# Gate/up projections of a SwiGLU layer as 2x2 block products with seven multiplications, and the down projection in pieces between them

## The chip, the cores and the metric

The kernel runs on one core of a Trainium2 chip. The metric is the device time of one execution in microseconds. In the texts, PE is TensorE, DVE is VectorE, ACT is ScalarE and SP is SyncE, whose queue issues the loads.

## The reference

A decoder trunk of two layers over 512 tokens and 1024 channels, in float32. Layer 0 mixes tokens by retention and pooling, layer 1 by a convolution module; each is followed by a SwiGLU sub-layer, and a final RMS norm ends the trunk. The change concerns SwiGLU alone (2816 hidden features):

```python
def rms_norm(x, g):
    y = x32 * lax.rsqrt(jnp.mean(x32 * x32, axis=-1, keepdims=True) + EPS)
    return (y * g).astype(x.dtype)

def swiglu(h, w_gate, w_up, w_down):
    return (jax.nn.silu(h @ w_gate) * (h @ w_up)) @ w_down

for layer in range(DEPTH):
    ...
    h = h + swiglu(rms_norm(h, ffn_norm_g[layer]), ffn_w_gate[layer], ffn_w_up[layer], ffn_w_down[layer])
return rms_norm(h, final_norm_g)
```

## The kernel before

Activations lie feature-major: X holds 8 tiles of 128 features by 512 tokens. A float32 product is made from fp32r parts. Each operand is split into a high part, a cast on ACT (L180 for weights, L230 for hidden tiles), and a low part, the difference to the original on DVE (L183, L231). A product is then three matmuls, high by high, high by low and low by high (`mm3`, L197 to L200).

Weights come in chunks of at most 128 x 2048 floats. `start_load` loads a chunk on SP's queue into `wr` (two buffers), `split_load` makes `wh` and `wl`, and `chunk(name, j)` splits one chunk ahead of the one it returns. A gate/up chunk holds 8 tiles of input features, each with 128 gate columns and 128 up columns, for one tile of hidden features; there are 22 of them. `feature_major` (L202) runs through it: 8 input tiles, two halves, three matmuls of 512 columns each, 48 in all, into one PSUM tile `ps_gu` of two banks. PSUM has three such pairs (`pair`, L302), and tiles for small results beside them.

`hidden` (L536) evacuates the pair: DVE multiplies both halves by the spread inverse rms (L539), ACT applies silu to the gate half (L540), DVE multiplies by the up half (L541), and the result is split into `hh` and `hl`. The inverse rms itself comes from token sums after chunk 0 (`inv_rms`, L294) and is spread over the partitions during chunk 1.

The hidden features go in two halves of 11 tiles. After 11 chunks the down projection of that half follows: four pairs of output tiles, each 2 x 11 x 3 matmuls of 512 columns into `ps_dn`, added to X on DVE (`add_residual`, L305). After layer 0's second half the add also prepares the next layer's input (`norm_input`, L241). After layer 1's, `finish` (L574) does the last pair in halves of 256 tokens, turns X back to token-major by transposes, and scales and stores the rows.

The order of instructions on each engine comes from a scheduler, in a few stretches from the order of the code (`manual_schedule`). An instruction waits for others by counters, at most some per instruction; each engine runs its instructions in order.

Of the kernel before, what the change touches and what calls it, by code (L numbers as in the profile page):

```python
# [22 lines left out]
DFF = 2816  # L23
FT = DFF // P
FH = FT // 2
CW = 31
EPS = 1e-6
CHUNK = 2048
# [52 lines left out]
def trunk(ctx: ExitStack, tc: tile.TileContext, a: dict):  # L81
# [17 lines left out]
    def V(name, i=0, n=1):  # L99
        o, _ = _VEC[name]  # L100
        return vec[:, o + i:o + i + n]
# [24 lines left out]
    for layer in range(2):  # L126
        if layer:
            plan += [("w_pw1", i, 8, 256) for i in range(8)]
            plan += [("w_pw2", i, 8, 256) for i in range(4)]
        for half in range(2):  # L130
            plan += [(f"w_gu{layer}", half * FH + i, 8, 256) for i in range(FH)]
            plan += [(f"w_dn{layer}", half * 8 + i, FH, 128) for i in range(8)]
    ready = {}
    state = {"started": 0, "next": 0, "used": 0}

# [2 lines left out]
    def start_load():  # L138
# [19 lines left out]
                nc.sync.dma_start(raw[:, s], a[name][j][:, s])  # L158
        raws[i] = raw

    def split_load(pieces=1, apart=False):
# [10 lines left out]
        wh = wp.tile([P, CHUNK], F32R, tag="wh", name=f"wh{i}")  # L172
        wl = wp.tile([P, CHUNK], F32R, tag="wl", name=f"wl{i}")
        ready[(name, j)] = (wh[:, :n].rearrange("p (k c) -> p k c", c=c),
                            wl[:, :n].rearrange("p (k c) -> p k c", c=c))
        pieces = KT if i == 0 else 4 if i == 1 else pieces
        step = n // pieces
        for k in range(pieces):
            s = slice(k * step, (k + 1) * step)
            nc.scalar.copy(wh[:, s], raw[:, s])  # L180
            if apart:
                yield
            nc.vector.tensor_tensor(wl[:, s], raw[:, s], wh[:, s].bitcast(F32), ALU.subtract)  # L183
            if i == 0:
                norm_input(k, vg[:, k:k + 1], None, xin)
            yield
# [118 lines left out]
    def add_residual(j, ps, gain=None, acc=None, bias=None):  # L305

        xx = X[:, 2 * j:2 * j + 2, :]
        if bias is None:
            nc.vector.tensor_tensor(xx, ps, xx, ALU.add)  # L309
# [12 lines left out]
    def both(ap):  # L322
        return ap.unsqueeze(1).to_broadcast([P, 2, S])
# [200 lines left out]


    def ffn(layer, acc, gain):
        with tc.tile_pool(name=f"hp{layer}", bufs=FH + 2, reuse_waits="tile") as hp:
            return ffn_in(layer, acc, gain, hp)

    def ffn_in(layer, acc, gain, hp):  # L530
        nacc = None
        row = {}
        for half in range(2):
            hh, hl = [], []

            def hidden(ps):  # L536
                t = wk.tile([P, 2, S], F32, tag="gu", name="gu")
                s = wk.tile([P, S], F32, tag="act", name="act")
                nc.vector.tensor_tensor(t, ps, both(row["rb"]), ALU.mult)  # L539
                nc.scalar.activation(s, t[:, 0, :], AF.Silu)  # L540
                nc.vector.tensor_tensor(s, s, t[:, 1, :], ALU.mult)  # L541
                hh.append(hp.tile([P, S], F32R, tag="hh", name=f"hh{len(hh)}"))
                hl.append(hp.tile([P, S], F32R, tag="hl", name=f"hl{len(hl)}"))
                split(hh[-1], hl[-1], s)

            pss = []
            for f in range(FH):
                wh, wl = chunk(f"w_gu{layer}", half * FH + f)
                pss.append(pair(f"ps_gu{f}"))
                late = {}  # L550
                if not half and f == 1:
                    r = inv_rms(acc)
                    late = {5: lambda: row.update(rb=spread(r, "rms"))}
                feature_major(pss[-1], wh, wl, xgh, xgl, between=late)
                while pss and row:
                    hidden(pss.pop(0))
            if half:
                nacc = new_acc()
            for j in range(3 if gain is None and half else 4):
                ps = pair(f"ps_dn{j}")  # L560
                for i in range(2):
                    down(ps, i, *chunk(f"w_dn{layer}", half * 8 + 2 * j + i), hh, hl)
                add_residual(j, ps, gain, nacc)
        if gain is None:
            finish(hh, hl, nacc)
        return nacc

    def down(ps, i, wh, wl, hh, hl, cols=FULL, between={}):
        for f in range(FH):
            if f in between:  # L570
                between[f]()
            mm3(ps[:, i, cols], wh[:, f, :], wl[:, f, :], hh[f][:, cols], hl[f][:, cols], f == 0, f == FH - 1)

    def finish(hh, hl, acc):  # L574

        A, B = HALVES
        for k in range(6):
            nc.scalar.activation(X[:, k, :], X[:, k, :], AF.Identity, scale=V("fin_g", k))
        ps = pair("ps_dn3")
        pts, stats = {}, {}  # L580

        def tail_add(i, cols):

            x = X[:, 6 + i, cols]
            nc.vector.tensor_tensor(x, ps[:, i, cols], x, ALU.add)
            sq = wk.tile([P, S // 2], F32, tag="sq", name="sqf")
            nc.scalar.activation(sq, x, AF.Square)
            nc.vector.tensor_scalar_mul(x, x, V("fin_g", 6 + i))
            return sq

        def turn(t, ks):

            if t not in pts:
                pts[t] = pair(f"ps_x{t}")
            for k in ks:
                nc.tensor.transpose(pts[t][:, k // 4, k % 4 * P:(k % 4 + 1) * P], X[:, k, t * P:(t + 1) * P], ident)

        def sums(cols, sqs):
# [18 lines left out]
        w6 = chunk("w_dn1", 14)  # L617
        w7 = chunk("w_dn1", 15)
        down(ps, 0, *w6, hh, hl, A)
        s6 = tail_add(0, A)  # L620
        down(ps, 1, *w7, hh, hl, A)
        s7 = tail_add(1, A)

        def at3():
            sums(A, [s6, s7])
            turn(0, range(8))

        def at6():
            turn(1, range(8))

        down(ps, 0, *w6, hh, hl, B, {3: at3, 6: at6})
        scale_rows(A)
        s6 = tail_add(0, B)
        down(ps, 1, *w7, hh, hl, B)
        s7 = tail_add(1, B)
        sums(B, [s6, s7])
        for t in (2, 3):
            turn(t, range(8))
        scale_rows(B)
# [331 lines left out]
```

## Time and profile before

| | |
|---|---|
| median of 3 runs | 1117.32 us (1116.86 to 1117.76) |
| the profiled execution | 1117.25 us |
| its span | 1115.1 us |
| granted PE clock, mean | 0.995 |
| DVE busy | 580.1 us in 784 instructions |
| ACT busy | 334.8 us in 383 instructions |
| load of a gate/up chunk, issue to landing | 4.8 us for 1024 KB, 44 of them |
| HBM read | 100.34 MB, 92 GB/s over the span |

The profile is one execution taken by the hardware profiler. Its span is what lies between the first and the last instruction; 2.15 us of the execution's time lie outside it. A row of a group gives busy time, the mean of one in nanoseconds, and the idle time of the engine just before. Matmuls are pipelined, so the length of one matmul in a row is longer than the distance to the next start. Layer 0's FFN has its first chunk from about 187 us to 198 us, layer 1's from about 738 us to 749 us; both end with the start of the next part, at 548 us and with the tail.

### The profile page before, as it was taken

The numbers are of one execution on the slowest core, as the hardware profiler recorded it, in microseconds if no ns is written. First come the engines' busy times: TensorE is split into PE (matmuls) and PEld (weight loads), VectorE is DVE, ScalarE is ACT, GpSimd is POOL, SyncE is SP. The second block draws the span as 40 slices with busy tenths as digits, with TensorE's granted clock in tenths as the row PEclk, the third lists the DMA queues.
The fourth block names the chain that finished last, engine by engine and source line by source line (L and its number), as shares of the span: only waits on it lengthen the run. The fifth ranks groups of instructions, "written<-read, shape, count | busy, mean of one in ns | idle before, by whom it ended". The sixth has DMA issues, their size and how long they took to land.

```text
span 1115.1 us, 12874 instructions
## 1 busy us (share of the span) xinstructions
PE 1100.3 (99%) x5504; PEld 896.3 (80%) x5504; DVE 580.1 (52%) x784; ACT 334.8 (30%) x383; POOL 20.1 (2%) x10
## 2 busy tenths in 40 slices
PE   9999999999999999999999999999999999999996
PEld 6877878888888888888886577988888888888886
DVE  7875646444432353434469857854444324344333
ACT  6622143223221132223332123432322112222331
POOL 0000100000000000000000410000000000000000
PEclk9999999999999999999999999999999999999998
DMA  8322113222223322222426562233221232231212
GB/s 280 124 93 96 38 44 139 82 101 88 78 78 128 113 81 108 89 79 81 149 76 118 100 137 77 76 114 110 79 102 57 99 136 93 101 110 55 91 65 76
DMA packets 24744, 109.89 MB, mean 99 GB/s; under 512 B 2800, under 2 KB 6768, under 8 KB 15984
## 3 DMA queue, kind: packets, MB, share of 16 engines
q1 hardware_dynamic: 24112, 108.03, 30.0%
q8 instruction: 43, 0.70, 0.3%
q10 hardware_dynamic: 576, 1.05, 0.3%
q14 instruction: 13, 0.11, 0.0%
HBM read 100.34 MB, written 2.10 MB: 92 GB/s over the span
## 4 chain that ended last, share of the span: by engine, by line
PE 91%; DVE 6%; issue 1%; DMA 1%; ACT 1%; SPq 0%; DVEq 0%; ACTq 0%
PE ps_gu L198 14%; PE ps_gu L199 14%; PE ps_gu L200 14%; PE ps_dn L200 7%; PE ps_dn L198 7%; PE ps_dn L199 7%; DVE d L693 3%; PE ps_c L701 2%; PE ps_pw L198 1%; PE ps_wo L199 1%; PE ps_qk L199 1%; PE ps_qk L200 1%; PE ps_wo L200 1%; PE ps_qk L198 1%; PE ps_pw L199 1%; PE ps_pw L200 1%
## 5 line engine op out<-in xcount | busy, mean ns | idle before, releaser
L180 ACT CAST wh<-wr 128x2048 fp32r<-128x2048 f32 (+4 forms) x116 | 179.8, 1554 | 505.9 <-PE ps_gu L199 240.1
L198 PE MATMUL ps_gu<-xgh,wh 128*128 128x512 f32 x704 | 274.4, 390 | 0.0
L200 PE MATMUL ps_gu<-xgh,wl 128*128 128x512 f32 x704 | 274.1, 389 | 0.0
L199 PE MATMUL ps_gu<-xgl,wh 128*128 128x512 f32 x704 | 274.1, 389 | 0.0
L183 DVE TENSOR_TENSOR wl<-wr,wh 128x2048 fp32r<-128x2048 f32 (+4 forms) x116 | 214.2, 1850 | 100.6 <-ACT wh L180 100.2
L539 DVE TENSOR_TENSOR gu<-ps_gu,bc_rms 128x1024 f32<-128x1024 f32 x44 | 53.9, 1225 | 210.8 <-PE ps_gu L200 202.7
L200 PEld LDWEIGHTS ps_gu<-xgh,wl 128*128 128x128 f32 x704 | 132.2, 188 | 27.5
L198 PEld LDWEIGHTS ps_gu<-xgh,wh 128*128 128x128 f32 x704 | 132.2, 188 | 27.3
L199 PEld LDWEIGHTS ps_gu<-xgl,wh 128*128 128x128 f32 x704 | 132.2, 188 | 27.2
L198 PE MATMUL ps_dn<-hh,wh 128*128 128x512 f32 (+1 forms) x374 | 141.3, 378 | 0.0
L200 PE MATMUL ps_dn<-hh,wl 128*128 128x512 f32 (+1 forms) x374 | 140.9, 377 | 0.0
L199 PE MATMUL ps_dn<-hl,wh 128*128 128x512 f32 (+1 forms) x374 | 140.9, 377 | 0.0
L198 PEld LDWEIGHTS ps_dn<-hh,wh 128*128 128x128 f32 x374 | 70.4, 188 | 12.9
L199 PEld LDWEIGHTS ps_dn<-hl,wh 128*128 128x128 f32 x374 | 70.4, 188 | 12.9
L200 PEld LDWEIGHTS ps_dn<-hh,wl 128*128 128x128 f32 x374 | 70.4, 188 | 12.8
L198 PE MATMUL ps_pw<-xgh,wh 128*128 128x512 f32 (+1 forms) x160 | 56.6, 354 | 0.0
L230 ACT CAST hh<-act 128x512 fp32r<-128x512 f32 x44 | 27.3, 621 | 96.4 <-DVE act L541 96.4
L199 PE MATMUL ps_pw<-xgl,wh 128*128 128x512 f32 (+1 forms) x160 | 55.9, 349 | 0.0
L200 PE MATMUL ps_pw<-xgh,wl 128*128 128x512 f32 (+1 forms) x160 | 55.8, 349 | 0.0
L309 DVE TENSOR_TENSOR X<-ps_dn,X 128x1024 f32<-128x1024 f32 x15 | 18.4, 1225 | 66.2 <-PE ps_dn L200 66.2
L231 DVE TENSOR_TENSOR hl<-act,hh 128x512 fp32r<-128x512 f32 x44 | 30.5, 693 | 30.2 <-ACT hh L230 30.2
L701 PE MATMUL ps_c<-R,dg 128*32 128x512 f32 (+1 forms) x512 | 43.9, 496 | 1.6 <-DMA R<-u 1.6
(188 smaller groups left out, 1181.5 us busy)
## 6 DMA issues: line engine op xcount, KB each, us to landing
wr<-in_w_gu SPq DMA_DIRECT2D x44, 1024.0 KB, 4.8
wr<-in_w_dn SPq DMA_DIRECT2D x32, 704.0 KB, 4.0
wr<-in_w_pw SPq DMA_DIRECT2D x12, 1024.0 KB, 4.9
R<-u SPq DMA_DIRECT2D x16, 270.0 KB, 8.0
wr<-in_w_o SPq DMA_DIRECT2D x4, 1024.0 KB, 4.7
X<-in_xT SPq DMA_DIRECT2D x8, 256.0 KB, 4.3
wr<-in_w_qk SPq DMA_DIRECT2D x2, 1024.0 KB, 5.1
wr<-in_w_u SPq DMA_DIRECT2D x2, 1024.0 KB, 4.8
```

Of the source, the lines that this page charges most:

```text
L180: nc.scalar.copy(wh[:, s], raw[:, s])
L183: nc.vector.tensor_tensor(wl[:, s], raw[:, s], wh[:, s].bitcast(F32), ALU.subtract)
L198: nc.tensor.matmul(out, lhsT=wh, rhs=xh, start=start, stop=False)
L199: nc.tensor.matmul(out, lhsT=wh, rhs=xl, start=False, stop=False)
L200: nc.tensor.matmul(out, lhsT=wl, rhs=xh, start=False, stop=stop)
L230: nc.scalar.copy(h, src)
L231: nc.vector.tensor_tensor(l, src, h.bitcast(F32), ALU.subtract)
L309: nc.vector.tensor_tensor(xx, ps, xx, ALU.add)
L539: nc.vector.tensor_tensor(t, ps, both(row["rb"]), ALU.mult)
L693: nc.vector.scalar_tensor_tensor(o, us[j][:, at], V("dwc", CW * j + q), o, ALU.mult, ALU.add)
L701: nc.tensor.matmul(ps[32 * i:32 * i + 32, :n], lhsT=dgs[j][:, i, g, :], rhs=Rs[j][:, i, 4 * g + cols.start:4 * g + cols.stop], start=g == ...
```

## The change

Of each layer's 22 gate/up chunks, 3 stay as they are (`NSTD`). The other 19 are computed as a 2x2 block product. One side is the weight chunk: its two halves of input features (4 tiles each) by gate and up. The other is the input: the same halves of features by two halves of 256 tokens. Seven products of blocks (4 tiles, 3 matmuls each, 256 columns, 84 matmuls) take the place of eight. Three use plain blocks of weights, four use sums of blocks.

Added work, per layer once: `prepare` makes the sums of input blocks `th`, `tl` (ACT scales, DVE subtracts, both split), and `last_operand` overwrites half of four input tiles with the last one. Per chunk: `plain_hi`, `plain_lo` (L594, L600) split the plain blocks; `add_up` (L606) makes the four sums of weight blocks in place in the loaded chunk, one after the other; `sums_hi`, `sums_lo` (L615, L620) split them.

The products gather in two PSUM tiles, `ps_xz` with x in its first bank and z in its second, and `ps_y`. x is accumulated through four products, and between them ACT copies what it holds at that point to SBUF (`sn`); DVE adds these up (L755 adds z, L758, L762) and scales by the inverse rms (L764, L765, L768).

The down projection is cut into six groups of 3, 4, 4, 3, 4 and 4 hidden tiles. Each group by each of the four output pairs is one piece, 24 in all. One piece follows each of the 19 block-product chunks, for the group whose hidden tiles are done; 5 pieces come at the end. A piece's sum is subtracted from X by `add_piece` at the start of the next cycle (before: one add for 11 tiles). Each piece loads its own slice of the down weights (`load_dn`, two DMAs) and splits it (`dn_hi`, `dn_lo`, L636, L641). Loads of chunks (`load_gu`) and pieces go through SP's queue. PE, DVE and ACT run in the order of the code throughout the FFN. In layer 1 the last two pieces are done in token halves with the tail.

The core of the diff, the cycle of one chunk:

```diff
+        def cycle(f, before):
+            s = f - first
+            xz, y = pair(f"ps_xz{f}"), pair(f"ps_y{f}")
+            x, z, y = xz[:, 0, :HS], xz[:, 1, :HS], y[:, 0, :HS]
...
+            product(x, plain_of(f, 0), whole(0, A), True)
+            nc.scalar.copy(sn[0][:, 0, :], x)
+            before()
+            product(y, sum_of(f, 1), part(0), True)
+            dn_hi(s, 0)
+            nc.scalar.copy(sn[1][:, 0, :], y)
+            product(x, sum_of(f, 2), part(1), False)
+            dn_hi(s, 1)
+            nc.scalar.copy(sn[0][:, 1, :], x)
+            plain_lo(f + 1)
+            product(z, plain_of(f, 1), whole(4, A), True)
+            add_up(f + 1)
+            dn_lo(s)
+            load_dn(s + 2)
+            nc.vector.tensor_tensor(g[:, 0, A], z, sn[0][:, 0, :], ALU.add)
+            product(x, sum_of(f, 3), part(2), False)
+            nc.scalar.copy(sn[1][:, 1, :], x)
+            nc.vector.tensor_tensor(g[:, 1, B], sn[1][:, 1, :], sn[1][:, 0, :], ALU.add)
+            sums_hi(f + 1, 1)
+            sums_hi(f + 1, 3)
+            product(y, sum_of(f, 4), whole(4, B), False)
+            nc.vector.tensor_tensor(g[:, 0, B], y, sn[0][:, 1, :], ALU.add)
+            sums_hi(f + 1, 2)
+            nc.vector.tensor_tensor(g[:, 0, :], g[:, 0, :], rb, ALU.mult)
+            nc.vector.tensor_tensor(g[:, 1, B], g[:, 1, B], rb[:, B], ALU.mult)
+            sums_hi(f + 1, 4)
+            product(x, plain_of(f, 2), whole(0, B), False)
+            nc.vector.tensor_tensor(g[:, 1, A], x, rb[:, A], ALU.mult)
+            nc.scalar.activation(sil, g[:, 0, :], AF.Silu)
+            sums_lo(f + 1)
+            load_gu(f + 3)
+            plain_hi(f + 2)
+            ps = piece(s)
+            if f == FT - 1:
+                weights(s + 1)
+            store_hidden(f, sil, g[:, 1, :])
+            return lambda: add_piece(s, ps)
```

What each chunk asks of the sums and products, and the way in:

```diff
+        def add_up(f):
+            if f < FT:
+                a11, a21, a12, a22 = [block(raw_g[f], half, r) for half in range(2) for r in range(2)]
+                for o, i in ((a22, a21), (a21, a11), (a11, a22), (a12, a11)):
+                    nc.vector.tensor_tensor(o, o, i, ALU.add)
...
+        def product(out, w, xs, first):
+            h, l = w
+            for k in range(4):
+                xh, xl = xs(k)
+                for n, (u, v) in enumerate(((h, xh), (h, xl), (l, xh))):
+                    nc.tensor.matmul(out, lhsT=u[:, k, :], rhs=v, start=first and k == 0 and n == 0,
+                                     stop=k == 3 and n == 2, skip_group_check=True)
...
+        feature_major(p0, *w, xgh, xgl)
+        prepare(0)
+        w = chunk(f"w_gu{layer}", 1)
+        load_gu(NSTD)
+        r = inv_rms(acc)
+        prepare(1)
+        p1 = pair("ps_gu1")
+        feature_major(p1, *w, xgh, xgl, between={5: lambda: row.update(rb=spread(r, "rms"))})
+        prepare(2)
+        prepare(3)
+        hidden(0, p0)
+        w = chunk(f"w_gu{layer}", 2, 0)
+        load_gu(NSTD + 1)
+        p2 = pair("ps_gu2")
+        feature_major(p2, *w, xgh, xgl)
+        plain_hi(NSTD)
+        plain_lo(NSTD)
+        add_up(NSTD)
+        for i in (1, 2, 3, 4):
+            sums_hi(NSTD, i)
+        hidden(1, p1)
+        sums_lo(NSTD)
+        load_gu(NSTD + 2)
+        last_operand()
+        plain_hi(NSTD + 1)
+        hidden(2, p2)
+        before = lambda: None
+        for f in range(NSTD, FT):
+            before = cycle(f, before)
```

How this moves instructions shows in the built order. First DVE, in the middle of layer 0's FFN. Before, a chunk has four instructions there: the gain on the PSUM pair `ps_gu`, the low part `wl` of the next weights, the product with the silu, and the low part `hl`:

```order
L539 TENSOR_TENSOR gu<-ps_gu_1913,bc_rms 128x1024
L183 TENSOR_TENSOR wl_1974<-wr_1971,wh_1973 128x2048
L541 TENSOR_TENSOR act<-act,gu 128x512
L231 TENSOR_TENSOR hl_1968<-act,hh_1967 128x512
L539 TENSOR_TENSOR gu<-ps_gu_1977,bc_rms 128x1024
```

Now one cycle, from add_piece (X and `ps_dn`) over the next chunk's plain low parts (here `wl`), its four sums (`wg`), the piece's low weights (`dl0d`) and the add of z (L755) to the low part of `hl`:

```order
L311 TENSOR_TENSOR X<-X,ps_dn_2087 128x1024
L600 TENSOR_TENSOR wl_2084<-wg_6_1928,wh_2083 128x1024
L600 TENSOR_TENSOR wl_2084<-wg_6_1928,wh_2083 128x512
L606 TENSOR_TENSOR wg_6_1928<-wg_6_1928 128x4x128 x4
L641 TENSOR_TENSOR dl0d_2144<-dr_2_1874,dh0d_2143 128x2x384
L755 TENSOR_TENSOR gu<-ps_xz_2111,sn_2113 128x256
L758 TENSOR_TENSOR gu<-sn_2114 128x256
L762 TENSOR_TENSOR gu<-ps_y_2112,sn_2113 128x256
L764 TENSOR_TENSOR gu<-gu,bc_rms 128x512
L765 TENSOR_TENSOR gu<-gu,bc_rms 128x256
L768 TENSOR_TENSOR gu<-ps_xz_2111,bc_rms 128x256
L620 TENSOR_TENSOR wl_2199<-wg_6_1928,wh_2198 128x2048
```

The evacuation, which stood first after a chunk, is now in pieces, and the first of them stands behind eight instructions that belong to the piece before, the next chunk and this piece's weights.

Second, PE at the change from z's product to x's third product, in the next cycle (`ps_xz` holds both, `th` and `tl` are sums of input blocks). The wait at the head of the third product is for DVE, and its count is reached with L755 of the same cycle; the wait at the head of z's product is for ACT's copy of x:

```order
L682 MATMUL ps_xz_2264<-xgh_1460,wh_2083 128x256 [waits Activation_49]
L682 MATMUL ps_xz_2264<-xgl_1461,wh_2083 128x256
L682 MATMUL ps_xz_2264<-xgh_1460,wl_2084 128x256
...
L682 MATMUL ps_xz_2264<-xgh_1482,wl_2084 128x256
L682 MATMUL ps_xz_2264<-th_0_1572,wh_2198 128x256 [waits DVE_49]
L682 MATMUL ps_xz_2264<-tl_0_1573,wh_2198 128x256
```

Before, the same place of PE's order has one chunk after another with no wait between them but for the buffers:

```order
L198 MATMUL ps_gu_2041<-xgh_1342,wh_1973 128x512
L199 MATMUL ps_gu_2041<-xgl_1343,wh_1973 128x512
L200 MATMUL ps_gu_2041<-xgh_1342,wl_1974 128x512
L198 MATMUL ps_gu_2041<-xgh_1460,wh_1973 128x512
L199 MATMUL ps_gu_2041<-xgl_1461,wh_1973 128x512
```

So PE now stops inside a chunk for two other engines, which it did not.

Third, DVE on the way into layer 0's FFN, after the last input tile (`xgl_1483`) is made. Before, the next work after four small clears for the convolution is the inverse rms (`ms` and on):

```order
L227 SCALAR_TENSOR_TENSOR xgl_1483<-X,vec,xgh_1482 128x512
L256 TENSOR_TENSOR acc<-acc,sq_1486 128x512
L661 MEMSET u_3780 128x31
L661 MEMSET u_3787 128x31
L661 MEMSET u_3849 128x31
L661 MEMSET u_3918 128x31
L296 TENSOR_SCALAR ms<-ps_ms 128x4
```

Now a prepare (`xr`, then `t4` in the row L666, then `tl`) and the split of chunk 2 (`wl_1579`) stand ahead of it:

```order
L229 SCALAR_TENSOR_TENSOR xgl_1483<-X,vec,xgh_1482 128x512
L258 TENSOR_TENSOR acc<-acc,sq_1486 128x512
L661 TENSOR_TENSOR xr_1565<-xg_1564 128x2x256
L663 SCALAR_TENSOR_TENSOR xr_1565<-xr_1565,xg_1564 128x256
L666 SCALAR_TENSOR_TENSOR t_0_1570<-xr_1565,xg_1564 128x256
L233 TENSOR_TENSOR tl_0_1573<-xr_1565,th_0_1572 128x768
L185 TENSOR_TENSOR wl_1579<-wr_1576,wh_1578 128x2048
L298 TENSOR_SCALAR ms<-ps_ms 128x4
```

So the inverse rms comes behind five instructions more, and three more prepares follow it before the evacuation of chunk 0.

More of the change, by code (lines that the diff above doesn't have):

```diff
@@ L25 @@
 FH = FT // 2
+NSTD = 3
+GROUPS = [range(h + i, h + j) for h in (0, FH) for i, j in ((0, 3), (3, 7), (7, 11))]
 CW = 31
@@ L129, in trunk @@
             plan += [("w_pw2", i, 8, 256) for i in range(4)]
-        for half in range(2):
-            plan += [(f"w_gu{layer}", half * FH + i, 8, 256) for i in range(FH)]
-            plan += [(f"w_dn{layer}", half * 8 + i, FH, 128) for i in range(8)]
+        plan += [(f"w_gu{layer}", i, 8, 256) for i in range(NSTD)]
     ready = {}
@@ L159, in start_load, with split_tiles @@
         raws[i] = raw
+    def split_tiles(i):
+        return [wp.tile([P, CHUNK], F32R, tag=f"{t}{i % 2}", name=f"{t}{i}", bufs=1) for t in ("wh", "wl")]
     def split_load(pieces=1, apart=False):
@@ L303, in pair, with add_residual @@
         return pmm.tile([P, 2, S], F32, tag="mm", name=name)
-    def add_residual(j, ps, gain=None, acc=None, bias=None):
+    def add_residual(j, ps, gain=None, acc=None, bias=None, sign=ALU.add):
         xx = X[:, 2 * j:2 * j + 2, :]
         if bias is None:
-            nc.vector.tensor_tensor(xx, ps, xx, ALU.add)
+            nc.vector.tensor_tensor(xx, xx, ps, sign)
         else:
@@ L526, in ffn @@
     def ffn(layer, acc, gain):
[L527 to L531, printed above, removed]
-        row = {}
[L533 to L563, printed above, removed]
-        if gain is None:
-            finish(hh, hl, nacc)
-        return nacc
@@ L568, in down @@
[L568 to L574, printed above, removed]
+        with tc.tile_pool(name=f"fx{layer}", bufs=1, reuse_waits="tile") as fx, \
+                tc.tile_pool(name=f"fg{layer}", bufs=1, reuse_waits="tile") as fg, \
+                tc.tile_pool(name=f"fy{layer}", bufs=1, reuse_waits="tile") as fy, \
+                tc.manual_schedule(engines={mybir.EngineType.PE, mybir.EngineType.DVE, mybir.EngineType.Activation}):
+            gap = fg.tile([P, 16], F32, name=f"gap{layer}")
+            nc.vector.memset(gap[:1, :1], 0.0)
+            return ffn_in(layer, acc, gain, fx, fy)
```

253 lines of the change are left out of this document (225 added, 28 removed).

## The prediction

> **What bounds the kernel now.** I read the page first: busy times, then the chain that ended last.
>
> ```profile
> PE 1100.3 (99%) x5504; PEld 896.3 (80%) x5504; DVE 580.1 (52%) x784; ACT 334.8 (30%) x383; POOL 20.1 (2%) x10
> ...
> PE 91%; DVE 6%; issue 1%; DMA 1%; ACT 1%; SPq 0%; DVEq 0%; ACTq 0%
> ```
>
> PE is busy for 99% of the span and is 91% of the chain; DVE has half its time free. Next the waits, for PE alone. The longest is its first row:
>
> ```profile
> PE ps_c L701 <- DMA R<-u: 1.6, 1, 1.6
> ```
>
> So PE waits nowhere for long, and taking matmul time away pays only if it still waits nowhere afterwards. What a matmul costs on the path is the distance between starts, since its 390 ns overlap the next one. The timeline of PE near the end has both widths side by side, 512 columns and then 256 (start, length):
>
> ```profile
> 1071.63 0.39 PE L198 MATMUL ps_dn<-hh,wh 128*128 128x512 f32 x1
> ...
> 1083.64 0.39 PE L200 MATMUL ps_dn<-hh,wl 128*128 128x512 f32 x1
> 1083.87 0.28 PE L198 MATMUL ps_dn<-hh,wh 128*128 128x256 f32 x1
> ...
> 1087.70 0.28 PE L200 MATMUL ps_dn<-hh,wl 128*128 128x256 f32 x1
> ```
>
> 53 steps in 12.01 us are 0.2266 us for 512 columns; 32 steps in 3.83 us are 0.1197 us for 256, a little over half.
>
> **Part 1, the matmuls.** A chunk of gate/up is 48 matmuls of 512 columns now, 48 x 0.2266 = 10.88 us. As seven block products it is 7 x 4 x 3 = 84 of 256 columns, 10.05 us. The down projection keeps its matmuls. So 0.83 us a chunk: 19 chunks give 15.7 us a layer, 31.4 us in both. An eighth fewer multiplications has become 7.6%, because narrow matmuls cost more per column.
>
> **Part 2, one cycle of a chunk.** The other engines' durations, from the groups by form (mean ns of one after the comma):
>
> ```profile
> L539 DVE TENSOR_TENSOR gu<-ps_gu,bc_rms 128x1024 f32<-128x1024 f32 x44 | 53.9, 1225 | 210.8 <-PE ps_gu L200 202.7 <-ACT bc_rms L291 8.1
> L309 DVE TENSOR_TENSOR X<-ps_dn,X 128x1024 f32<-128x1024 f32 x15 | 18.4, 1225 | 66.2 <-PE ps_dn L200 66.2
> L183 DVE TENSOR_TENSOR wl<-wr,wh 128x2048 fp32r<-128x2048 f32 x66 | 151.3, 2292 | 44.7 <-ACT wh L180 44.5
> L183 DVE TENSOR_TENSOR wl<-wr,wh 128x1024 fp32r<-128x1024 f32 x2 | 2.4, 1220 | 0.0
> L183 DVE TENSOR_TENSOR wl<-wr,wh 128x512 fp32r<-128x512 f32 x8 | 5.2, 686 | 0.1
> L585 DVE TENSOR_TENSOR X<-ps_dn,X 128x256 f32<-128x256 f32 x4 | 1.7, 421 | 7.2 <-PE ps_dn L200 7.2
> L667 DVE SCALAR_TENSOR_TENSOR u<-gu,vec,act 128x256 f32<-128x256 f32 x4 | 1.9, 484 | 1.3 <-ACT act L665 1.2
> L180 ACT CAST wh<-wr 128x2048 fp32r<-128x2048 f32 x66 | 126.2, 1912 | 329.3 <-PE ps_gu L199 192.2 <-PE ps_dn L199 28.9 <-PE ps_g L449 28.0
> L180 ACT CAST wh<-wr 128x1024 fp32r<-128x1024 f32 x2 | 2.0, 1042 | 0.0
> L180 ACT CAST wh<-wr 128x512 fp32r<-128x512 f32 x8 | 4.5, 612 | 3.8 <-PE ps_p L219 3.8
> L540 ACT ACTIVATE act<-gu 128x512 f32<-128x512 f32 x44 | 27.5, 626 | 3.6 <-DVE gu L539 2.6
> L226 ACT ACTIVATE xgh<-X,vec 128x512 fp32r<-128x512 f32 x24 | 17.2, 716 | 1.9 <-DVE X L309 1.6
> L291 ACT COPY mus<-ps_mu 128x256 f32<-128x256 f32 x2 | 0.7, 372 | 8.5 <-PE ps_mu L287 8.5
> ```
>
> How they follow each other is in the timelines: DVE back to back, DVE on its own result, ACT back to back, DVE after PE, and PE after a wait.
>
> ```profile
> 192.89 0.75 DVE L227 SCALAR_TENSOR_TENSOR xgl<-X,vec,xgh 128x512 fp32r<-128x512 f32 x1
> 193.55 0.69 DVE L256 TENSOR_TENSOR acc<-acc,sq 128x512 f32<-128x512 f32 x1
> ...
> 199.74 0.16 DVE L269 TENSOR_TENSOR rs_t<-rs_t,rs_h 128x4 f32<-128x4 f32 x1
> 199.94 0.16 DVE L270 SCALAR_TENSOR_TENSOR rs_y<-rs_t,rs_y 128x4 f32<-128x4 f32 x1
> ```
>
> ```profile
> 714.49 1.14 ACT L180 CAST wh<-wr 128x512 fp32r<-128x512 f32 x2
> ```
>
> ```profile
> 221.37 0.39 PE L200 MATMUL ps_gu<-xgh,wl 128*128 128x512 f32 x1
> 221.80 1.22 DVE L539 TENSOR_TENSOR gu<-ps_gu,bc_rms 128x1024 f32<-128x1024 f32 x1 [4.84 <-PE ps_gu L200]
> ```
>
> ```profile
> 685.78 0.39 PE L221 MATMUL ps_p<-zh,wh 128*128 128x256 f32 x1 [0.60 <-DVE zh L756]
> 686.00 0.28 PE L222 MATMUL ps_p<-zh,wl 128*128 128x256 f32 x1
> ```
>
> Independent work on DVE starts 0.09 us before the last ends; dependent work 0.04 after. A second 512 cast on ACT adds 0.52. A hop between engines is 0.03 to 0.05, counted from the end of the last matmul, and PE's first step after a wait is 0.22.
>
> The kernel text decides the rest. x and z are the two halves of one PSUM tile, and in the built order waits go by tile: z's product waits for ACT's copy of x, and x's third product waits for DVE's add of z (L755). DVE reaches that add only behind add_piece, the low parts of the next chunk's plain blocks, four block sums each waiting for the one before, and the low part of the piece's weights. So I count from the end of one add of z to the next.
>
> - PE restarts at 0.05; x's third product takes 0.22 + 11 x 0.12 = 1.54, y's second 1.44 (to 3.03, results 3.19), x's fourth 1.44 (to 4.47, results 4.63). Then the piece: 18 matmuls (3 chunks) to 8.55, or 24 (4 chunks) to 9.91; results 0.16 later.
> - ACT: four casts of sums, which wait for y's second: 3.22 + 3 x 0.52 + 0.61 = 5.4.
> - DVE: adds and gains up to 5.08, low part of the sums 5.43 to 7.72, product with the silu to 8.33; ACT's cast of hh to 8.98; low part hl to 9.70.
> - DVE then: add_piece from 9.62 (3 chunks) or, waiting for PE, 10.10 (4). To the end of the next add of z: 1.14 + 1.14 + 0.73 + 3 x 0.73 + 0.60 + 0.87 (1.14 for 4 chunks, 0.95 and 1.22 less the overlap) + 0.42 = 7.1 or 7.3.
>
> The period is 16.7 us (3 chunks) or 17.4 us (4). PE's own work is 84 x 0.1197 + 18 x 0.2266 = 14.13, or 15.49. PE waits 2.5 or 1.95 us in every cycle. From chunk 3 to chunk 21 there are 18 such steps, 8 with 3 chunks and 10 with 4, the last 0.4 shorter because nothing is prepared: 8 x 2.55 + 10 x 1.95 - 0.4 = 39.5 us a layer. DMA adds no wait: load_gu has a cycle for its transfer, and load_dn's two smaller ones on SP stand ahead of it.
>
> **Part 3, the way in.** The first chunks now also carry four prepare steps, in order on DVE and ACT. The timelines and the chain where layer 0's FFN starts:
>
> ```profile
> 197.93 1.90 ACT L180 CAST wh<-wr 128x2048 fp32r<-128x2048 f32 x1 [6.00 <-PE ps_gu L199]
> ...
> 206.80 0.59 ACT L291 COPY bc_rms<-ps_rms 128x512 f32<-128x512 f32 x1 [6.97 <-PE ps_rms L287]
> ```
>
> ```profile
> 198.94 0.16 DVE L296 TENSOR_SCALAR ms<-ps_ms 128x4 f32<-128x4 f32 x1 [4.54 <-PE ps_ms L279]
> ...
> 203.21 0.16 DVE L270 SCALAR_TENSOR_TENSOR rs_y<-rs_t,rs_y 128x4 f32<-128x4 f32 x1
> ...
> 749.77 0.16 DVE L296 TENSOR_SCALAR ms<-ps_ms 128x4 f32<-128x4 f32 x1 [5.12 <-PE ps_ms L279]
> ```
>
> ```profile
> 198.12 0.79 PE ps_ms L279 x8
> ...
> 205.87 0.89 PE ps_rms L287 x8
> ```
>
> Chunk 2's weights can be split only when chunk 0 is done: ACT to 199.83, DVE to 202.2; the twelve small steps of rsqrt (4.4 us between the quoted two, of which the 2.2 us of a split stood among them) to 204.4. A prepare is 0.69 + 2 x 0.52 = 1.73 on DVE, then ACT's cast (0.83, between 512 and 1024) and the next two scaled copies (0.62 + 0.72), because its two buffers rotate. Prepare 1 to 206.1, ACT's rms copy and copies to 208.7, prepare 2 to 210.4, prepare 3 to 213.8, its low part to 215.1. hidden(0), 1.2 + 0.63 + 0.75 + 0.62 + 0.69 with hops, to 219.1; plain low parts to 221.2; four sums to 224.1; hidden(1) to 228.0; low part of the sums to 230.3. PE finished chunk 2 at 198.91 + 2 x 10.88 + 0.89 = 221.56, and y's first product stands until 230.3. Then four low parts of the last operand (231.6), hidden(2) (235.6, with ACT's copy of x behind it), plain low parts (237.3), sums (240.1), piece weights (241.0), and the add of z ends at 241.4. PE's own work would have had z at 221.56 + 5.75 = 227.3: 14.1 us late. Layer 1 has the same rows 550.8 us later, so again 14.1.
>
> **Part 4, the ends.** In the last four pieces of layer 0 (5.44 us of PE each) DVE has an add, two norms and a split, about 6 us; the low weights come 0.6 late twice: 1.2. In layer 1 piece 23's weights queue behind the squares and come 2.0 late, and the tail has a 512 add for a 256 one and a second square: 0.65.
>
> **Sum.** 2 x (-15.7 + 14.1 + 39.5) + 1.2 + 2.65 = +79.7 us. The profiled execution took 1117.25 us, its span 1115.1 and 2.15 around it; the median is 1117.32. So 1117.25 + 79.7 = 1197 us.
>
> **Bounds.** The uncertain terms are not PE's. Below: if the hidden split never delays the next add_piece, a 3-chunk cycle has only the stretch behind the piece's end, 8.71 + 7.1 = 15.8, and if a 4-chunk one is 0.25 shorter, the 18 steps cost 30; with a way in of 11 us that is 2 x (-15.7 + 11 + 30) = +51, 1168. Above: 12 hops of the loop each 0.06 longer are 0.7 a cycle, 25 us: 1222.
>
> **The rivals.**
> *The wait is not there, faster.* If x's third product can run while z is read, PE waits only on the way in. Without the wait at L755 the copy of x frees PE at 235.2 there, and z, x, y, x and the piece follow: 10.5 us late instead of 14.1. Then 1117.25 - 31.4 + 21 + 3.9 = 1111 us. It decides where DVE's stretch from the piece's end to the add of z is under 5.74 us, PE's four products, plus 0.83, the gain per chunk, so 6.6 against 7.1 and 7.3 here. For it: x and z lie in different banks, and the margin is under a microsecond. Against: every term of the stretch is a measured row, and the wait is in the built order. 0.09. The Trainium skill, Perfetto Trace Analysis, Matmuls, has independent groups rotate through different PSUM banks so that the evacuation of one overlaps the next group's matmuls; by that rule this case comes true, and no row here shows PE held by a neighbouring bank's reader.
>
> *No way-in loss either, faster still.* If the prepare steps fit beside chunks 0 to 2: 1117.25 - 31.4 + 3.9 = 1090 us. Against: in part 3 DVE and ACT take turns from 198 to 241 us without a free microsecond. 0.02.
>
> *The waits also cost clock, slower still.* After a stretch in which PE stood 1.5 us, the windows show the granted clock (PEclk) below 1.00:
>
> ```profile
> 620.00:632.00 12.00, 10.54 (x77) 5.51 (x69) 11.93 (x16) 0.69 (x1) 4.78 (x2) 1.00 0.40 102
> 632.00:650.00 18.00, 18.00 (x147) 10.18 (x150) 11.17 (x16) 5.60 (x7) 1.92 (x1) 0.91 0.67 122
> ```
>
> 0.09 x 18 us is 1.6 us lost. In all 36 cycles that is 58 us: 1255 us. At the two ways in alone it is within the range. Against: PE still works 14.13 of 16.7 us in a cycle. 0.03. The Trainium skill, TensorE: Matmul & The Clock Gate, HAM oscillation, wants no PE gaps above about 3.4 us; only the 7-us wait of the way in would break that.
>
> *It does not do what it says.* The built order has the 84 narrow matmuls, so this gets nothing.
>
> **How the numbers follow.** The forecast has 0.86. A measurement here tells 0.2% (2.2 us) from no change. Faster: 0.11, the two rivals. Same: 0.01. Slower: 0.88. The range 1165 to 1222 is the forecast's bounds; the rivals outside hold 0.14.
>
> **What would show it.** Right: PE busy falls to about 90%; the waits list PE on DVE gu (L755) with 1 to 2 us, 38 times, and once a layer on the low part of the sums (L620) with 7; cycles of 16.7 and 17.4 us; 256-column steps of 0.12. Wrong: L755 before z's results are out, or cycles of 14.1 and 15.5 us.

## The result and the profile after

The changed kernel takes 1200.4 us (median of 4 runs, 1200.19 to 1205.47), the kernel before 1117.52 us beside it: a ratio of 1.0754, 95% interval 1.0725 to 1.0782. It is slower by 83 us; the forecast was 1197.

The profiled execution is the longest of the four, 1205.47 us with a span of 1203.6. The page's busy row and the chain that ended last (PEld is PE's weight load; issue is time in which the engine waits for nothing that the profile shows):

```profile
PE 1099.2 (91%) x6854; PEld 947.7 (79%) x6854; DVE 862.2 (72%) x1290; ACT 480.5 (40%) x830; POOL 20.9 (2%) x10
...
PE 68%; DVE 22%; issue 4%; ACT 3%; DMA 2%; SPq 0%; ACTq 0%; DVEq 0%
```

PE's busy time is where it was (1100.3 before), but its share of the span has gone from 99% to 91%, and in the chain from 91% to 68%. Most of what it lost there, DVE has gained: 6% before, 22% now. The unchanged busy time doesn't mean that the products save nothing: the same matmuls of a cycle with a piece of 3 chunks count 14.5 us of busy time here and 13.93 in the run below that has no waits in its cycles (1074.2 us in all). The list of PE's waits (total us, times, longest) says for whom:

```profile
PE ps_xz L682 <- DVE gu L755: 50.1, 38, 1.9
PE ps_xz L682 <- ACT sn L749: 18.4, 38, 1.3
PE ps_y L682 <- DVE wl L620: 8.8, 2, 4.4
PE ps_xz L682 <- ACT sn L742: 4.7, 2, 2.3
PE ps_y L682 <- DVE gu L710: 4.0, 2, 2.0
PE ps_ta L200 <- DVE X L868: 2.6, 1, 2.6
```

The first row is the wait in every cycle, once for each of the 38 block chunks: x's third product for the add of z. In most cycles it is 1.1 or 1.6 us. The second is z's product waiting for ACT's copy of x out of the same tile. The next three come once a layer, on the way in; the last belongs to the tail.

How one cycle closes on itself shows in DVE's timeline from one add of z to the next (start, length; in brackets the idle time before and who ended it):

```profile
274.81 0.41 DVE L755 TENSOR_TENSOR gu<-ps_xz,sn 128x256 f32<-128x256 f32 x1
277.40 0.43 DVE L758 TENSOR_TENSOR gu<-sn 128x256 f32<-128x256 f32 x1 [2.18 <-ACT sn L757]
278.42 0.42 DVE L762 TENSOR_TENSOR gu<-ps_y,sn 128x256 f32<-128x256 f32 x1 [0.59 <-PE ps_y L682]
...
280.57 2.29 DVE L620 TENSOR_TENSOR wl<-wg,wh 128x2048 fp32r<-128x2048 f32 x1 [0.31 <-ACT wh L615]
...
284.15 0.69 DVE L233 TENSOR_TENSOR hl<-act,hh 128x512 fp32r<-128x512 f32 x1 [0.69 <-ACT hh L232]
284.76 1.21 DVE L311 TENSOR_TENSOR X<-X,ps_dn 128x1024 f32<-128x1024 f32 x1
...
290.53 0.95 DVE L641 TENSOR_TENSOR dl0d<-dr,dh0d 128x768 fp32r<-128x768 f32 x1
291.40 0.41 DVE L755 TENSOR_TENSOR gu<-ps_xz,sn 128x256 f32<-128x256 f32 x1
```

The idle times all lie ahead of `hl`. DVE waits 2.18 us right after the add, because PE, just released, must first make the products that DVE needs next. From `hl` on it works without a pause, 284.15 to 291.40, while PE comes to its wait at the other end:

```profile
289.96 0.28 PE L682 MATMUL ps_xz<-xgh,wl 128*128 128x256 f32 x1
291.87 0.38 PE L682 MATMUL ps_xz<-th,wh 128*128 128x256 f32 x1 [1.63 <-DVE gu L755]
```

z's last matmul starts at 289.96; DVE is then at the chained sums, with the weights' low part (L641) still between it and the add. The two engines take turns, each idle while the other is due.

### The profile page after: what moved, and what is told of

Read it like the earlier page. It is cut to its first block, busy times and chain, and to the rows that moved or that the text cites. A ratio compares the mean times of both kernels' runs of the same rounds, so it can differ in the third digit from the quotient of the medians.

```text
span 1203.6 us, 16770 instructions
## 1 busy us (share of the span) xinstructions
PE 1099.2 (91%) x6854; PEld 947.7 (79%) x6854; DVE 862.2 (72%) x1290; ACT 480.5 (40%) x830; POOL 20.9 (2%) x10
## 4 chain that ended last, share of the span: by engine, by line
PE 68%; DVE 22%; issue 4%; ACT 3%; DMA 2%; SPq 0%; ACTq 0%; DVEq 0%
PE ps_xz L682 16%; PE ps_y L682 7%; PE ps_dn L200 6%; PE ps_dn L202 6%; PE ps_dn L201 6%; DVE wg L606 4%; DVE d L995 3%; DVE X L311 2%; DVE el L600 2%; DVE wl L600 2%; PE ps_c L1003 1%; DVE gu L755 1%; PE ps_wo L201 1%; DVE dl0d L641 1%; PE ps_qk L201 1%
## 5 line engine op out<-in xcount | busy, mean ns | idle before, releaser
L682 PE MATMUL ps_xz<-th,wh 128*128 128x256 f32 x304 | 92.2, 303 | 54.8 <-DVE gu L755 50.1
L606 DVE TENSOR_TENSOR wg<-wg 128x512 f32<-128x512 f32 x152 | 105.2, 692 | 5.2
L615 ACT CAST wh<-wg 128x512 fp32r<-128x512 f32 x152 | 83.1, 617 | 45.9 <-PE ps_y L682 40.0
L620 DVE TENSOR_TENSOR wl<-wg,wh 128x2048 fp32r<-128x2048 f32 x38 | 87.1, 2292 | 11.6 <-ACT wh L615 11.6
L185 DVE TENSOR_TENSOR wl<-wr,wh 128x2048 fp32r<-128x2048 f32 (+3 forms) x47 | 75.0, 1606 | 18.2 <-ACT wh L182 18.2
L682 PE MATMUL ps_xz<-th,wl 128*128 128x256 f32 x304 | 87.8, 289 | 0.0
L682 PE MATMUL ps_xz<-tl,wh 128*128 128x256 f32 x304 | 87.8, 289 | 0.0
L682 PE MATMUL ps_xz<-xgh,eh 128*128 128x256 f32 x240 | 69.5, 290 | 10.1 <-ACT sn L749 10.1
L758 DVE TENSOR_TENSOR gu<-sn 128x256 f32<-128x256 f32 x38 | 16.2, 425 | 86.7 <-ACT sn L757 86.7
L682 PE MATMUL ps_xz<-xgh,el 128*128 128x256 f32 x240 | 67.3, 280 | 0.0
L682 PE MATMUL ps_xz<-xgl,eh 128*128 128x256 f32 x240 | 67.3, 280 | 0.0
```

Source lines behind the costliest of these rows:

```text
L606: nc.vector.tensor_tensor(o, o, i, ALU.add)
L615: nc.scalar.copy(block(sums[f][0], *SUMS[i]), block(raw_g[f], *SUMS[i]))
L620: nc.vector.tensor_tensor(l, raw_g[f], h.bitcast(F32), ALU.subtract)
L682: nc.tensor.matmul(out, lhsT=u[:, k, :], rhs=v, start=first and k == 0 and n == 0, stop=k == 3 and n == 2, skip_group_check=True)
```

## The experiments

Theory 1 is the prediction's: x's third product waits for the add of z because both are halves of one tile, and DVE reaches that add late. Theory 2: DVE's total work, some 12.6 us a cycle, sets the cycle. Theory 3: the lost time is granted clock.

**z beside y.** x has a tile of its own; z is the second half of y's.

```diff
-            xz, y = pair(f"ps_xz{f}"), pair(f"ps_y{f}")
-            x, z, y = xz[:, 0, :HS], xz[:, 1, :HS], y[:, 0, :HS]
+            x, yz = pair(f"ps_x{f}"), pair(f"ps_yz{f}")
+            x, z, y = x[:, 0, :HS], yz[:, 1, :HS], yz[:, 0, :HS]
```

> The add of z stays where it is in VectorE's order; only z's place changes: it is the second half of y's PSUM tile, and x has a tile of its own. Theory 1 (x's third product waits for the add of z because both are halves of one tile): that product now waits only for ScalarE's copy of x, y's second product takes over the wait for the add, and the cycle is one product (1.44 us) shorter: periods of 15.2 and 16.0 us instead of 16.6 and 17.4, about 50 us less, 1148 us. Theory 2 (VectorE's total work sets the cycle, not the tile): periods and time stay, 1195 to 1205 us. Theory 3 (the lost time is the granted clock, the waits only its occasion): PE's idle time goes but the half-clock stretches stay, more than 1165 us.

Measured: 1143.17 us, ratio to the kernel before 1.0236 (1.0221 to 1.0251). The wait went one product further on, to y's second, and was half as long:

```profile
PE ps_yz L682 <- DVE gu L755: 25.6, 36, 1.3
```

The starts of two neighbouring adds in a cycle with a piece of 3 chunks, and in one with 4:

```profile
256.81 0.42 DVE L755 TENSOR_TENSOR gu<-ps_yz,sn 128x256 f32<-128x256 f32 x1
272.00 0.42 DVE L755 TENSOR_TENSOR gu<-ps_yz,sn 128x256 f32<-128x256 f32 x1
...
318.63 0.42 DVE L755 TENSOR_TENSOR gu<-ps_yz,sn 128x256 f32<-128x256 f32 x1
334.63 0.42 DVE L755 TENSOR_TENSOR gu<-ps_yz,sn 128x256 f32<-128x256 f32 x1
```

15.19 and 16.00 us: 1.4 less than the 16.61 and 17.43 of the changed kernel, one product. DVE's order and work are unchanged, so theory 2 falls with this run. So does theory 3 as the whole of the loss: it had more than 1165 us.

**The add of z early.** The tile is shared as in the changed kernel; the add moves ahead of the four sums and of `dn_lo`.

```diff
             product(z, plain_of(f, 1), whole(4, A), True)
+            nc.vector.tensor_tensor(g[:, 0, A], z, sn[0][:, 0, :], ALU.add)
             add_up(f + 1)
             dn_lo(s)
             load_dn(s + 2)
-            nc.vector.tensor_tensor(g[:, 0, A], z, sn[0][:, 0, :], ALU.add)
```

> The tile stays shared; the add of z moves ahead of the four chained sums and of the down weights' low parts in VectorE's order. Theory 1: x's third product still waits for the add, but the add comes as soon as z's product is out, if VectorE is through with the piece's add and the plain low parts: periods of about 15.5 and 16.9 us, 1171 us. Theory 2 (VectorE's total work): nothing changes, 1195 to 1205 us, since VectorE does the same work in another order. Theory 3 (clock): PE waits less, half-clock stretches stay: more than 1185 us.

Measured: 1171.81 us, 1.049 (1.0472 to 1.0507). The add now waits for PE, and PE still for the add:

```profile
257.27 0.42 DVE L752 TENSOR_TENSOR gu<-ps_xz,sn 128x256 f32<-128x256 f32 x1 [2.38 <-PE ps_xz L682]
272.83 0.42 DVE L752 TENSOR_TENSOR gu<-ps_xz,sn 128x256 f32<-128x256 f32 x1 [2.37 <-PE ps_xz L682]
...
320.89 0.42 DVE L752 TENSOR_TENSOR gu<-ps_xz,sn 128x256 f32<-128x256 f32 x1 [3.45 <-PE ps_xz L682]
337.82 0.42 DVE L752 TENSOR_TENSOR gu<-ps_xz,sn 128x256 f32<-128x256 f32 x1 [3.45 <-PE ps_xz L682]
```

Periods of 15.56 and 16.93 us with DVE idle 2.4 and 3.5 us ahead of the add: DVE is not the bound any more, only the tile is. The same in the list of waits:

```profile
PE ps_xz L682 <- DVE gu L752: 22.5, 38, 0.7
PE ps_xz L682 <- ACT sn L749: 18.7, 38, 1.6
```

**Both.** The two edits together.

> z beside y and the add of z early, both. Theory 1: no product waits for VectorE within a cycle, the periods come to PE's own work of 14.1 and 15.5 us plus some tenths, and the time to 1125 to 1130 us: what is left against the kernel before is the way in and the ends, and it is no faster than before. Theory 2 (VectorE's total work, some 12.6 us a cycle, sets the cycle): 1195 to 1205 us. Theory 3 (clock): over 1150 us.

Measured: 1110.28 us, 0.9945 (0.9928 to 0.9963): half a per cent under the kernel before, which I had not expected. The list of PE's waits begins on the way in; no row of the cycle is left but one of 0.4 us:

```profile
PE ps_yz L682 <- DVE wl L620: 8.6, 2, 4.4
PE ps_x L682 <- ACT sn L742: 4.7, 2, 2.3
PE ps_yz L682 <- DVE gu L710: 4.0, 2, 2.0
```

The adds lie 13.93 us apart, and 15.40:

```profile
254.56 0.43 DVE L752 TENSOR_TENSOR gu<-ps_yz,sn 128x256 f32<-128x256 f32 x1 [0.74 <-PE ps_yz L682]
268.50 0.43 DVE L752 TENSOR_TENSOR gu<-ps_yz,sn 128x256 f32<-128x256 f32 x1 [0.75 <-PE ps_yz L682]
...
311.76 0.43 DVE L752 TENSOR_TENSOR gu<-ps_yz,sn 128x256 f32<-128x256 f32 x1 [1.95 <-PE ps_yz L682]
327.16 0.43 DVE L752 TENSOR_TENSOR gu<-ps_yz,sn 128x256 f32<-128x256 f32 x1 [1.95 <-PE ps_yz L682]
```

These are the cycles of PE alone. My 1125 to 1130 had put the waits of the 36 cycles at 70 to 75 us. From the first add of a layer to its last, the changed kernel takes 311.25 and 311.68 us, this one 265.46 and 265.47: 92 us.

**Without the four sums.** The tile and the order are the changed kernel's; four of the seven products take single blocks of weights in place of sums.

```diff
-                for o, i in ((a22, a21), (a21, a11), (a11, a22), (a12, a11)):
+                for o, i in ():
```

> The four chained sums of each chunk are left out, so that the weights of four of the seven products are single blocks and not sums; matrix work, copies and splits are the same in number and size. VectorE has 2.8 us less to do ahead of the add of z; tile and order stay. Theory 1: the add of z comes 1.2 to 2 us earlier and the wait for it shrinks to what PE, ScalarE's copy and the add itself make: periods of about 15.5 and 16.9 us, about 1170 us. Theory 2 (VectorE's total work): 2.8 us less a cycle, 36 x 2.8 = 100 us, down to PE's own periods, 1125 us. Rival on the weights' side (the sums are late for the next chunk's operands and the low parts of the sums at the cycle's end are what PE waits for): under 1165 us too, and the list of waits would have named L620.

Measured: 1166.66 us, 1.0439 (1.0424 to 1.0455).

```profile
PE ps_xz L682 <- DVE gu L755: 23.5, 38, 1.1
PE ps_xz L682 <- ACT sn L749: 18.4, 38, 1.3
```

The rows are close to those of the run with the early add, and the periods are the same, 15.57 and 16.93 us. The whole of DVE's 2.8 us a cycle, 100 us, buys 34. Theory 2 had 1125.

**One prepare in place of four.** `t4` and the sums of input group 0 stand in for the others, so the products take other numbers; their matmuls are the same in number and size.

```diff
+        th[1:], tl[1:] = [th[0]] * 3, [tl[0]] * 3
-        prepare(1)
...
-        prepare(2)
-        prepare(3)
```

> Three of the four preparations of the token operands are left out: the blocks of group 0 of the dimension stand in for those of groups 1 to 3, so the products are of other numbers; the number and size of matmuls, chunks and pieces are as in the changed kernel. Theory 1 (the way in is lost to ScalarE's and VectorE's preparation standing ahead of the first block chunk's weights): the first add of z comes some 7 us earlier than the changed kernel's 242.0 us, 14 us in two layers, about 1186 us, and the wait for the low parts of the sums (L620, 4.4 us) shrinks or goes. Theory 2 (the way in waits for something else: the first block chunk's weights from memory, or TensorE's half clock there): within 4 us of the changed kernel, 1196 to 1204 us.

Measured: 1184.65 us, 1.0597 (1.0583 to 1.0612), 15.75 less than the changed kernel. The first add of z starts at 233.82 us, where the changed kernel has it at 241.57: 7.75 us in layer 0. From the last add of layer 0 to the first of layer 1 it is 273.92 us and 280.94: 7.0. L620 and L710 are gone from the list; L742 is left, and longer:

```profile
PE ps_xz L682 <- DVE gu L755: 51.8, 38, 2.5
...
PE ps_xz L682 <- ACT sn L742: 5.7, 2, 2.8
```

So the way in is lost to preparation on DVE and ACT, and it adds up with the cycles' waits, which stay.

**Token halves in the kernel before.** Each chunk as 96 matmuls of 256 columns.

```diff
-                feature_major(pss[-1], wh, wl, xgh, xgl, between=late)
+                for cols in HALVES:
+                    feature_major(pss[-1], wh, wl, xgh, xgl, cols, late)
+                    late = {}
```

> The kernel before, but each gate/up chunk as two token halves, 96 matmuls of 256 columns in place of 48 of 512; nothing else. Theory 1 (the narrow step costs 0.1197 us, 0.006 more than half of a wide one's 0.2266): 0.61 us more for each of 44 chunks, 27 us, 1144 us. The cycles without waits just measured (13.93 us with 18 wide steps of 0.2266 and 84 narrow ones) speak for 0.1173 a step: 0.38 us a chunk, 1134 us. Rival (the narrow step costs its columns alone, and what the products save is lost elsewhere): 1117 to 1120 us. Rival (each narrow matmul waits for its weight load): 1160 us or more.

Measured: 1145.77 us, 1.0249 (1.0235 to 1.0263). PE waits nowhere that it did not before. DVE's evacuations, one behind each chunk, count the chunks:

```profile
224.41 1.22 DVE L539 TENSOR_TENSOR gu<-ps_gu,bc_rms 128x1024 f32<-128x1024 f32 x1 [5.39 <-PE ps_gu L200]
235.93 1.23 DVE L539 TENSOR_TENSOR gu<-ps_gu,bc_rms 128x1024 f32<-128x1024 f32 x1 [5.39 <-PE ps_gu L200]
```

11.52 us, 0.1200 a step, against 10.88: 0.64 x 44 = 28.2 us, and 28.5 were measured. Narrow matmuls alone cost what the prediction said.

**The way in.** Both mends, a fourth plain chunk, and the preparation spread out; the core of the edit is the way in:

```diff
-NSTD = 3
+NSTD = 4
...
         prepare(2)
-        prepare(3)
-        hidden(0, p0)
-        w = chunk(f"w_gu{layer}", 2, 0)
-        load_gu(NSTD + 1)
+        w = chunk(f"w_gu{layer}", 2)
+        load_gu(NSTD)
         p2 = pair("ps_gu2")
         feature_major(p2, *w, xgh, xgl)
+        prepare(3)
+        hidden(0, p0)
+        hidden(1, p1)
+        w = chunk(f"w_gu{layer}", 3, 0)
+        load_gu(NSTD + 1)
+        p3 = pair("ps_gu3")
+        feature_major(p3, *w, xgh, xgl)
...
-        hidden(1, p1)
+        weights(0)
+        hidden(2, p2)
         sums_lo(NSTD)
...
-        hidden(2, p2)
+        ps0 = piece(0)
+        hidden(3, p3)
```

> The kernel with both mends (z beside y, add of z early), and a fourth chunk of each layer left as one product, with the preparations spread over chunks 0 to 2, the first piece of the down projection moved ahead of the first block chunk, the last pieces' weights prepared ahead of the squares, and the last rows' scales made in two parts. Theory 1 (what is left against the pure saving is the way in and the ends): 18 cycles a layer each 0.92 to 1.03 us under the kernel before, 35 us in all, less about 4 for what remains of the ends: 1087 us, the list of waits without L620 and L742. Theory 2 (the preparation costs its time wherever it stands, since ScalarE and VectorE are full there): 1100 to 1112 us, with waits on VectorE or ScalarE at new places in chunks 0 to 4.

Measured: 1097.2 us, 0.9813 (0.9799 to 0.9826). Neither theory's figure: L620 is gone and L742 down to 0.4 us, but a new wait stands in the first piece, for the hidden chunk 2, twice:

```profile
PE ps_dn L200 <- ACT hh L232: 4.1, 2, 2.0
```

Behind it the windows (length, busy time of PE, PEld, DVE, ACT and POOL, then the granted clock PEclk, the DMA share and GB/s) show something more:

```profile
234.40:236.80 2.40, 0.36 (x3) 0.01 (x1) 0.96 (x3) 1.31 (x3) 0.00 (x0) 0.96 0.51 164
236.80:240.10 3.30, 3.30 (x7) 2.38 (x8) 3.30 (x4) 2.64 (x6) 0.00 (x0) 0.51 0.00 0
240.10:244.00 3.90, 3.90 (x30) 3.64 (x29) 2.73 (x5) 1.01 (x2) 0.00 (x0) 1.00 0.80 267
```

In the 2.40 us up to 236.8 PE is busy for 0.36; the wait itself is 2.0 us. When PE starts again the clock is a half for 3.3 us: 7 wide matmuls where 14 would have gone. In layer 1 a stand of the same length is followed by 6.8 us at half clock (776.2 to 783.0, PEclk 0.52). Just ahead of each stand lies a shorter wait, for the piece's low weights, of 0.4 to 0.5 us.

**Without that stand.** The first piece's weights come ahead of the hidden chunks, chunks 0 and 1 of the hidden are interleaved, chunk 2 comes ahead of the sums.

```diff
         prepare(3)
-        hidden(0, p0)
-        hidden(1, p1)
+        for i in range(2):
+            dn_hi(0, i)
+        up = [hidden_up(p) for p in (p0, p1)]
+        up = [hidden_act(*u) for u in up]
+        for f in range(2):
+            split_hidden(f, up[f])
+        dn_lo(0)
+        load_dn(2)
...
         plain_lo(NSTD)
+        up = hidden_up(p2)
         add_up(NSTD)
+        up = hidden_act(*up)
...
-        weights(0)
-        hidden(2, p2)
+        split_hidden(2, up)
```

> The version before it (both mends, fourth plain chunk) let PE stand 2.4 us in the first piece of each layer, for hidden chunk 2, and the granted clock then was a half for 3.4 us in layer 0 and 6.8 us in layer 1. Here the first piece's weights are made ahead of the hidden chunks, chunks 0 and 1 of the hidden are made interleaved, and chunk 2 ahead of the four sums; the same instructions otherwise. Theory 1 (the stand itself, 2.4 us, brings the half clock about): stand and half clock go, 4.8 + 5.1 = about 10 us, 1088 us. Theory 2 (the half clock there has another cause): 4.8 us, 1092 us, and the half-clock stretches stay. Theory 3 (VectorE is full there and the stand moves to the sums' low parts, ahead of y's first product): 1095 to 1099 us, L620 in the list of waits.

Measured: 1086.5 us, 0.9725 (0.9712 to 0.9738). The stretches around the first pieces of the two layers, in the windows:

```profile
231.40:240.00 8.60, 8.60 (x50) 7.55 (x49) 6.76 (x10) 5.10 (x11) 0.00 (x0) 1.00 0.37 122
760.00:776.00 16.00, 16.00 (x91) 14.01 (x90) 13.53 (x18) 9.01 (x19) 0.00 (x0) 1.00 0.25 88
```

No stand, and the clock is full. 10.7 us came back. The waits on the first pieces were 4.9 of them (2.0 and 0.4 to 0.5 in each layer), and half clock over 3.3 and 6.8 us makes another 4.9, as theory 1 had it. This version is 31 us faster than the kernel before and 114 faster than the changed one.

## Why the prediction was right

**Part 1, the matmuls, held.** The narrow step was put at 0.1197 us and is 0.1200 in the run with token halves. In the products it is a little less: (13.93 - 18 x 0.2266) / 84 = 0.1173, so a chunk saves 0.92 to 1.03 us and not 0.83. That is some 5 us over both layers that I left out, and that only the kernels without the waits get in full.

**Part 2, the cycle, held in mechanism and size.** Periods of 16.7 and 17.4 us were predicted, 16.61 and 17.43 are the common ones. The last cycle of a layer was misread: it was to be 0.4 us shorter because nothing is prepared. In layer 1 it is shorter (16.92), but in layer 0 DVE then splits a weight chunk for the next part, for which it waits on ACT's cast, and the cycle is 18.30:

```profile
549.47 2.29 DVE L185 TENSOR_TENSOR wl<-wr,wh 128x2048 fp32r<-128x2048 f32 x1 [3.22 <-ACT wh L182]
```

The other steps fall where they were put: with the add's end, 275.22, as zero, the low part of the sums runs from 5.35 to 7.64 (predicted 5.43 to 7.72), hl ends at 9.62 (9.70), and the next add of z ends at 16.59 (16.7). What the experiments add is how the two causes share the loss. Over the cycle without waits (13.93 and 15.40), the shared tile alone costs 1.6 and 1.5 us (the runs with the early add, and without sums), the late add alone 1.3 and 0.6 (z beside y), both 2.7 and 2.0. Either mend leaves the other cause, and with both the loss is gone.

**Part 3, the way in, held in its sum.** The first add of z ends at 241.99 us (241.4), the low part of the sums at 230.84 (230.3):

```profile
226.03 0.36 PE L682 MATMUL ps_y<-th,wh 128*128 128x256 f32 x1 [1.96 <-DVE gu L710]
230.90 0.58 PE L682 MATMUL ps_y<-th,wl 128*128 128x256 f32 x1 [4.40 <-DVE wl L620]
235.74 0.58 PE L682 MATMUL ps_xz<-th,wh 128*128 128x256 f32 x1 [2.34 <-ACT sn L742]
```

y's first product was to stand once, 7 us at L620. It stands twice: first for hidden(1)'s evacuation (L710), which frees the pair that it writes to, then for the low part. The matmuls of 0.58 us between belong to a half clock, which I had not put there (a granted clock of 0.66 from 222 to 242 us). In layer 0 it moved nothing, since DVE goes from 236.06 to the add of z without a pause.

In layer 1 the three waits are the same: 2.02, 4.40 and 2.33 us.

**Part 4, the ends,** came out in layer 1 for the most part, and not in layer 0. In layer 0 the low weights were to come late twice, 1.2 us in all; but behind the last cycle's wait, which ends at 553.29, PE waits for nothing up to 600 us. In layer 1 the sum had 2.65 us for late weights and a wider add, and PE does stand 2.6 us there (`ps_ta`, L868): PE is through at 1175.45, the low weights end at 1177.30 and the add behind them at 1177.91. A wait of 2.5 us for the last squares (`ps_fs`, 0.4 before) was not in the sum. No run changed the ends alone.

**What was missed is clock within the cycles.** Here are the windows of three consecutive stretches of the changed kernel's layer 0, four cycles, one, and one:

```profile
241.90:308.30 66.40, 58.05 (x408) 53.55 (x408) 50.58 (x69) 28.69 (x56) 0.00 (x0) 1.00 0.28 92
308.30:327.30 19.00, 17.38 (x108) 16.02 (x108) 13.08 (x19) 7.33 (x14) 0.00 (x0) 0.91 0.25 84
327.30:344.70 17.40, 15.86 (x108) 14.50 (x108) 13.00 (x18) 7.32 (x14) 0.00 (x0) 1.00 0.28 91
```

The middle one has the same matmuls as the last, a clock of 0.91, and is 1.5 us longer (18.94 from add to add against 17.41). Five of the 36 periods are so, 7.5 us. They are most of what the profiled execution has over 1197 (8.5 us). That it is 5 us longer than the three others for the same reason is argued only from their mean clock, 0.982 to 0.985 against 0.979; they left no trace. The rival that gave the waits a price in clock had its mechanism right; it had it in all 36 cycles, at 1.6 us each, and it came in five. That the median is within 4 us of 1197 is in part luck, since the terms that were left out have both signs: this clock, the last cycle and the last squares on one side, what the changed kernel gets of the 5 us of part 1 and the 1.2 of part 4 on the other.

**The rivals' figures came true elsewhere.** "The wait is not there" gave 1111 us, and with the tile and the add mended 1110.28 were measured. "No way-in loss either" gave 1090, and 1086.5 were measured, with one block chunk a layer fewer. So the large terms of the sum hold to a few microseconds (closer agreement is chance, since the rivals' sums lack the 5 us of part 1), and the wait that the first rival wanted away was there for the reason given. The Trainium skill, Perfetto Trace Analysis, Matmuls, has independent groups rotate through banks so that the evacuation of one overlaps the matmuls of the next. x and z did lie in different banks here, and PE still waited 50.1 us for z's reader, because in the built order waits go by tile. When x had its own tile that wait was gone. Whether PE could write x's bank while DVE reads z's in the same tile, without the wait, was not tried.

## What to carry to other kernels

Saving matmuls pays only where PE stays fed: put results that are read and results that are still being written in different tiles, and let the evacuation that frees PE stand first in the reader's queue, ahead of work for the next step. Price a loop by going once round the circle of engines from one event to the same event in the next turn, and see in which row an engine stops waiting. Where PE must stand, keep it short: behind a stand of two microseconds the clock cost 1.6 us more in one layer here and 3.3 in the other.

## What the runs showed of the hardware

- A wait of 2.0 us on the way in (the run that is named so) was followed by half clock (PEclk 0.51 and 0.52), for 3.3 us in one layer and 6.8 us in the other; with the wait gone, the clock was full. It is no fixed rule. With one prepare, PE waits 2.83 us for ACT's copy of x (L742) ahead of 227.99 in layer 0 and ahead of 810.16 in layer 1. Behind the first the clock is about a half, behind the second it is full:

```profile
228.00:231.40 3.40, 2.94 (x14) 2.64 (x15) 3.33 (x5) 1.41 (x4) 0.00 (x0) 0.57 0.00 0
810.20:813.60 3.40, 2.94 (x23) 2.73 (x24) 3.33 (x5) 1.38 (x4) 0.00 (x0) 1.00 0.02 5
```

  The Trainium skill, TensorE: Matmul & The Clock Gate, HAM oscillation, wants no gaps above about 3.4 us; here 2.0 us, with 0.4 to 0.5 us just ahead, came before a half clock in both layers. The same page (What's actually happening) has the clock judged in free-running windows of 3413 ns. The lengths of 3.3 and 6.8 us fit that, and so would the unequal fate of equal waits; no run tested it.
- In the cycles of the changed kernel the wait for the add is 0.6 to 1.9 us. The five cycles of 36 with the lower clock are those that begin behind a wait of 1.9 us, and it is a half clock for some 3.4 us:

```profile
308.74 0.51 PE L682 MATMUL ps_xz<-th,wh 128*128 128x256 f32 x1 [1.90 <-DVE gu L755]
308.70:312.10 3.40, 3.36 (x16) 3.36 (x17) 0.06 (x1) 0.37 (x1) 0.00 (x0) 0.52 0.48 154
```

  In each of the five the clock over the whole cycle is 0.91. Behind the waits of 1.7 us and less it happened in no cycle, nor with z beside y (0.45 to 1.3 us) or the early add (up to 0.7 us for the add). With one prepare, the wait of 1.9 us comes four times, and one of the four is followed by it. What picks that one is open.
- A 256-column step costs 0.120 us where a 512-column step costs 0.2266, and 0.1173 in the mean of the block products. What makes the difference between the two narrow figures was not tried.
